# Gate and up weights of two column tiles in one load, and two products side by side

## The chip, the cores and the metric

The kernel runs on one core of one Trainium2 chip. The metric is the device time of one execution in microseconds (us). The engines are called as in the profile: PE multiplies matrices, PEld is its loading of stationary operands, DVE, ACT and POOL work on vectors, SP issues the DMA transfers.

## The reference

One layer of a decoder over 2048 tokens of 1024 numbers: a projection, two groups of attention heads (a softmax group and a stick-breaking group), an output projection, and then a gated feed-forward network. The part that the change touches is that network:

```
f = rmsnorm(h, norm_ffn)
gate = einsum("bsd,df->bsf", f, w_gate)      # 1024 -> 2816
up   = einsum("bsd,df->bsf", f, w_up)        # 1024 -> 2816
h = h + einsum("bsf,fd->bsd", silu(gate) * up, w_down)
return rmsnorm(h, norm_final)
```

All of it is in float32. The kernel reaches that precision by splitting each operand into a high and a low part and adding three products.

## The kernel before, in words

The 2048 tokens are four blocks of 512. Each block passes four stages: P projects it, A is its attention, D its output projection, F its feed-forward network. Blocks 0 and 1 run F one at a time (`ffn`, L974); blocks 2 and 3 share one (`ffn_pair`, L1105), which has loads and products of its own and is not touched.

The code does not issue instructions. It records them as tasks, and `Plan.order` (L295) then writes the order of every engine by playing the tasks through a table of costs: whenever an engine is free, the ready task with the smallest key goes next. The key is a rank and then the place in the recording. Every instruction is issued from one helper, so all rows of the profile have the line L479; they are told apart by the names of their tiles. The order is fixed before the run: an engine whose next instruction must wait does not take the one behind it.

The ranks (L74 to L91) put the feed-forward network of block 0 beside the attention of blocks 2 and 3, at rank 2 like the attention of block 3 but later in the recording: its products (`ps_gu`, `ps_d`) fill the places where no product of the attention (`ps_s`, `pt`, `ot`, `po`) is ready. Block 1 follows, with the output projections of blocks 2 and 3 (`ps_t`, `ps_o`) between its steps; then the pair of blocks 2 and 3 (`ps_m`). What reads a sum out of the matrix engine's memory gets a key smaller by three (`ACC_FIRST`, L88).

The sums stand in eight banks. The attention reserves five of them while it has work (L49 to L51); the tiles of `acc_tile` (L796) share the others. They open in the order of recording, with one liberty: a tile may open ahead of up to ten that were recorded before it, unless one of those or itself is marked as one of a pair (L333 to L334).

`ffn` goes over the 22 column tiles of 128 columns, two at a time. For a tile, `gate_up` (L978) loads 1024 rows by 128 columns of the gate weights (`raw`, three buffers), splits them in two halves into high and low parts (`whi` on ACT, `wlo` on DVE, five buffers each), and adds 24 matmuls into one sum (`ps_gu`): eight row chunks, three products each. Then it does the same with the up weights. From the two sums come the sigmoid (ACT, `sg`), two multiplications (DVE, `sg`), the high part of the result (ACT, `hh`) and the low part (POOL, `hl`). After both tiles `down` (L932) adds, for each of eight output tiles, three matmuls of the first column tile and three of the second (`ps_d`, 48 in all), and DVE adds the sum to the block's accumulator (`acc`).

Of the kernel before, what the change touches and what calls it, by code (L numbers as in the profile page):

```python
# [12 lines left out]
F32 = mybir.dt.float32  # L13
F32R = mybir.dt.float32r
I32 = mybir.dt.int32
AF = mybir.ActivationFunctionType
ALU = mybir.AluOpType
# [4 lines left out]
P = 128  # L22
# [3 lines left out]
KC = D // P  # L26
TB = 512
# [31 lines left out]
SG_BUFS = 4  # L59
# [423 lines left out]
def layer(ctx, tc, x, positions, inv_freq, norm_mix, w_in, q_latent_norm, w_uq,  # L483
# [4 lines left out]
    def f32(ap):  # L488
        return ap.bitcast(F32)
# [23 lines left out]
    plan = Plan()  # L513
# [30 lines left out]
    def split_w(raw, hi, lo):  # L544
        plan.scalar.activation(hi, raw, AF.Copy)
        plan.vector.tensor_tensor(out=lo, in0=raw, in1=f32(hi), op=ALU.subtract)

    def mm3(ps, sh, sl, mh, ml, start, stop):
        plan.tensor.matmul(ps, lhsT=sh, rhs=mh, start=start, stop=False)
        plan.tensor.matmul(ps, lhsT=sh, rhs=ml, start=False, stop=False)  # L550
        plan.tensor.matmul(ps, lhsT=sl, rhs=mh, start=False, stop=stop)


    with ExitStack() as s:

        def planned(name, bufs):
            p = PlanPool(plan, s.enter_context(tc.tile_pool(name=name, bufs=bufs)), bufs)
            p.psum = False
            return p
# [8 lines left out]
        sp, tp, op, accp = [PlanPool(plan, psum, n) for n in (S_B, TP_B, O_B, None)]  # L568
# [227 lines left out]
        def acc_tile(shape, dtype, name, pair=False):  # L796
            tile_ = accp.tile(shape, dtype, tag="acc", name=name)
            tile_.base.pair = pair
            return tile_
# [12 lines left out]
        ew = planned("c_wk", 2)  # L812
# [21 lines left out]
        def weights(src, shape, parts=2):  # L834
            raw = wr.tile(shape, F32, tag="raw", name="raw")
            if isinstance(src, list):
                for i, part in enumerate(src):
                    plan.sync.dma_start(raw[:, i], part)
            else:
                plan.sync.dma_start(raw, src)  # L840
            res = []
            n = shape[1] // parts
            for i in range(parts):
                a = wp.tile([P, n] + shape[2:], F32R, tag="hi", name="whi")
                z = wp.tile([P, n] + shape[2:], F32R, tag="lo", name="wlo")
                split_w(raw[:, i * n:(i + 1) * n], a, z)
                res.append((a, z))
            return res
# [83 lines left out]
        def down(accs, order, hts, dws):  # L932

            for at in order:
                for dh in range(2):
                    ds_ = slice(dh * 512, (dh + 1) * 512)
                    for n in at:
                        ts_ = slice(n % BT * P, (n % BT + 1) * P)
                        ps = acc_tile([P, 512], F32, "ps_d")
                        for i in range(2):  # L940
                            hh, hl = hts[i][n // BT]
                            mm3(ps, hh[:, ts_], hl[:, ts_], dws[i][dh][0], dws[i][dh][1], i == 0, i == 1)
                        plan.vector.tensor_tensor(out=accs[n][:, ds_], in0=accs[n][:, ds_], in1=ps, op=ALU.add)

        def down_weights(c):
            return [weights(w_down[0, i * P:(i + 1) * P, :], [P, D]) for i in (c, c + 1)]

        def load_accs(blocks):
            accs = []
            for n, b in enumerate(blocks):  # L950
                for t in range(BT):
                    pool, tag = (apool, f"acc{t}") if n == 0 else (kv, "kv"[t % 2])
                    a = pool.tile([P, D], F32, tag=tag, name="acc")
                    plan.sync.dma_start(a, d_h[b * TB + t * P:b * TB + (t + 1) * P, :])
                    accs.append(a)
            return accs

        def last_norm(blocks, accs, order):
            pool, tag = (kv, "v") if blocks == [1] else (wr, "raw")
            gfin = pool.tile([P, D], F32, tag=tag, name="gfin")  # L960
            plan.sync.dma_start(gfin, norm_final.unsqueeze(0).broadcast_to([P, D]))
            for n in order:
                a = accs[n]
                so = small.tile([P, 2], F32, tag="so", name="so")
                for g in range(2):
                    squares(a[:, g * 512:(g + 1) * 512], so[:, g:g + 1])
                plan.vector.tensor_tensor(out=so[:, 0:1], in0=so[:, 0:1], in1=so[:, 1:2], op=ALU.add)
                ro = small.tile([P, 1], F32, tag="ro", name="ro")
                rstd_chain(small, so[:, 0:1], 1, D, ro)
                plan.vector.scalar_tensor_tensor(out=a, in0=a, scalar=ro, in1=gfin, op0=ALU.mult, op1=ALU.mult)  # L970
                g = blocks[n // BT] * BT + n % BT
                plan.sync.dma_start(out[0, g * P:(g + 1) * P, :], a)

        def ffn(b, between):  # L974

            fh, fl = sources[b]

            def gate_up(c):  # L978
                pss = []
                for src in (w_gate, w_up):  # L980
                    ws = weights(src[0, :, c * P:(c + 1) * P].rearrange("(c p) n -> p c n", p=P), [P, KC, P])
                    ps = acc_tile([P, TB], F32, "ps_gu")
                    for k in range(KC):
                        a, z = ws[k // 4]
                        mm3(ps, a[:, k % 4, :], z[:, k % 4, :], fh[k], fl[k], k == 0, k == KC - 1)
                    pss.append(ps)
                hh = hp.tile([P, TB], F32R, tag="hh", name="hh")
                hl = hp.tile([P, TB], F32R, tag="hl", name="hl")
                sg = ew.tile([P, TB], F32, tag="sg", name="sg", bufs=SG_BUFS)
                plan.scalar.activation(sg, pss[0], AF.Sigmoid)  # L990
                plan.vector.tensor_tensor(out=sg, in0=pss[0], in1=sg, op=ALU.mult)
                plan.vector.tensor_tensor(out=sg, in0=pss[1], in1=sg, op=ALU.mult)
                plan.scalar.activation(hh, sg, AF.Copy)
                plan.gpsimd.tensor_tensor(out=hl, in0=sg, in1=f32(hh), op=ALU.subtract)
                return [(hh, hl)]

            accs = []
            for c in range(0, NF, 2):
                hts = [gate_up(c), gate_up(c + 1)]
                dws = down_weights(c)  # L1000
                accs = accs or load_accs([b])
                down(accs, [[n] for n in range(BT)], hts, dws)
                for f in between.get(c // 2, ()):
                    f()
            plan.rank += NORM_LATE
            last_norm([b], accs, range(BT))
            plan.rank -= NORM_LATE
# [479 lines left out]
        for what in ORDER:  # L1487
            kind, blocks, between, rank = what[0], what[1], what[2] if len(what) > 2 else {}, RANKS["PADF".index(what[0])]
            rank = what[3] if len(what) > 3 else rank
            plan.rank = rank  # L1490
            steps = {}
            for at, other in between.items():
                todo = out_proj(int(other[1])) if other[0] == "D" else pair_steps
                for i, f in zip(at if isinstance(at, tuple) else (at,) * len(todo), todo):
                    steps.setdefault(i, []).append(f)
            if kind == "P":
                project(blocks, [f for fs in steps.values() for f in fs])
            elif kind == "A":
                plan.dense = False
                attention(blocks)  # L1500
                plan.dense = True
            elif isinstance(blocks, tuple):
                ffn_pair(blocks, ops, rest)
            else:
                sources[blocks], todo = ffn_input(blocks, t_tags)
                for f in todo:
                    f()
                ffn(blocks, steps)
# [26 lines left out]
```

## Time and profile before

| | us |
|---|---|
| median of 3 runs | 2981.82 (2981.56 to 2983.75) |
| the profiled execution | 2980.0 |
| its span | 2978.2 |
| PE busy in the span | 2938.2 (99%) |
| DVE busy | 2313.0 (78%) |
| ACT busy | 1779.5 (60%) |
| POOL busy | 514.4 (17%) |

The span is what the profile covers; the execution's own time is 1.8 us longer. A busy PE is one with a matmul under way, and a matmul is counted longer than the distance to the next one's start, so gaps shorter than that do not show as idle time.

### The profile page before, as it was taken

To read this page: it belongs to the slowest core of one execution; us is meant where nothing else is said; L and a number is where in the kernel's file an instruction comes from. 1 tells how busy PE (TensorE), PEld (TensorE's weight loads), DVE (VectorE), ACT (ScalarE), POOL (GpSimd) and SP (SyncE) were. 2 spreads that over 40 slices of the span, in tenths; PEclk is the share of its full clock that TensorE was granted. 3 is DMA by queue.
4 is the path that set the end of the run, shared out by engine and by line. 5 is a ranking of instruction groups with operands and counts; after the bars stand their busy time and mean duration, and the time that the engine had idled before them with its cause. 6 is when DMAs were issued, how large, how long until landed. Compare 5 with 4: busy or idle time off the path is not lost.

```text
span 2978.2 us, 46737 instructions
## 1 busy us (share of the span) xinstructions
PE 2938.2 (99%) x16308; PEld 2521.4 (85%) x16308; DVE 2313.0 (78%) x4448; ACT 1779.5 (60%) x3834; POOL 514.4 (17%) x487
## 2 busy tenths in 40 slices
PE   8999999999999999999999999999999999999998
PEld 7989889988888888888888888888887888888887
DVE  6668888886889879798979797555758777777777
ACT  6568878775767778777777786444534332233323
POOL 0011222220213213141414131000003101000101
PEclk9999999999999999999999999999999999999999
DMA  7988876669743445334333354546533311111212
GB/s 217 282 269 259 248 228 204 189 195 280 229 122 120 128 128 158 117 121 140 116 114 114 104 168 153 176 141 196 173 95 117 121 57 57 43 57 43 69 45 85
DMA packets 403426, 437.73 MB, mean 147 GB/s; under 512 B 76875, under 2 KB 296054, under 8 KB 403190
## 3 DMA queue, kind: packets, MB, share of 16 engines
q1 hardware_dynamic: 403190, 434.74, 47.8%
q8 instruction: 129, 2.11, 0.3%
q14 instruction: 107, 0.88, 0.1%
HBM read 350.78 MB, written 83.89 MB: 146 GB/s over the span
## 4 chain that ended last, share of the span: by engine, by line
PE 88%; DVE 5%; DMA 3%; ACT 2%; issue 1%; SPq 0%; POOL 0%; POOLq 0%; ACTq 0%; DVEq 0%
PE ps_gu L479 15%; PE ps_d L479 15%; PE ps_m L479 14%; PE ps_s L479 10%; PE ot L479 9%; PE pt L479 7%; PE ps_q L479 5%; PE ps_o L479 4%; PE ps_v L479 3%; PE ps_lat L479 2%; PE ps_t L479 1%; PE po L479 1%; DVE wlo L479 1%; DVE tb L479 1%; DVE acc L479 1%
## 5 line engine op out<-in xcount | busy, mean ns | idle before, releaser
L479 ACT ACTIVATE whi<-raw 128x512 fp32r<-128x512 f32 (+1 forms) x726 | 447.7, 627 | 574.8 <-PE ps_d L479 204.9
L479 DVE TENSOR_TENSOR wlo<-raw,whi 128x512 fp32r<-128x512 f32 (+1 forms) x726 | 515.0, 720 | 229.3 <-ACT whi L479 223.8
L479 POOL TENSOR_TENSOR p<-p,tb 128x512 f32<-128x512 f32 (+3 forms) x320 | 327.0, 1023 | 594.9 <-DVE tb L479 562.5
L479 DVE TENSOR_TENSOR pl<-pt,ph 128x512 fp32r<-128x512 f32 (+1 forms) x576 | 366.9, 651 | 45.7 <-ACT ph L479 42.8
L479 ACT ACTIVATE ph<-pt 128x512 fp32r<-128x512 f32 (+1 forms) x576 | 318.3, 580 | 132.3 <-PE pt L479 117.2
L479 PE MATMUL ps_s<-k,q 128*128 128x512 f32 (+3 forms) x1280 | 379.7, 374 | 3.0 <-DVE tb L479 3.0
L479 PE MATMUL pt<-diagonal,p 128*128 128x128 f32 x2176 | 358.8, 274 | 0.9 <-DVE pl L479 0.9
L479 PE MATMUL ps_m<-fop,whi 128*128 128x512 f32 (+1 forms) x1254 | 357.0, 373 | 0.0
L479 DVE TENSOR_TENSOR acc<-acc,ps_d 128x512 f32<-128x512 f32 x352 | 235.9, 682 | 71.1 <-PE ps_d L479 69.7
L479 PE MATMUL ps_gu<-th,whi 128*128 128x512 f32 x704 | 282.4, 401 | 0.0
L479 PE MATMUL ps_gu<-tl,whi 128*128 128x512 f32 x704 | 281.8, 400 | 0.0
L479 PE MATMUL ps_gu<-th,wlo 128*128 128x512 f32 x704 | 280.9, 399 | 0.0
L479 PE MATMUL ps_d<-whi,hh 128*128 128x512 f32 x704 | 277.5, 394 | 1.4 <-ACT hh L479 1.4
L479 PE MATMUL ps_d<-wlo,hh 128*128 128x512 f32 x704 | 277.2, 394 | 0.0
L479 PE MATMUL ps_d<-whi,hl 128*128 128x512 f32 x704 | 271.1, 393 | 0.0
L479 PEld LDWEIGHTS pt<-diagonal,p 128*128 128x128 f32 x2176 | 255.8, 141 | 14.3 <-issue 1.1
L479 PEld LDWEIGHTS ps_m<-fop,whi 128*128 128x128 f32 x1254 | 226.5, 188 | 44.8
L479 PEld LDWEIGHTS ps_s<-k,q 128*128 128x128 f32 x1280 | 222.8, 189 | 33.9 <-DVE tb L479 5.1
L479 DVE TENSOR_TENSOR_SCAN tb<-ps_s,tb,p 128x512 f32<-128x512 f32 x192 | 244.7, 1277 | 5.2 <-ACT ps_s L479 2.8
L479 PE MATMUL ot<-pl,v 128*128 128x256 f32 (+1 forms) x1152 | 244.5, 292 | 0.3
L479 PE MATMUL ot<-ph,v 128*128 128x256 f32 (+1 forms) x1152 | 233.6, 283 | 3.9 <-ACT ph L479 3.7
L479 DVE TENSOR_REDUCE m<-ps_s 128x1 f32<-128x512 f32 (+2 forms) x320 | 188.6, 605 | 58.4 <-PE ps_s L479 57.6
(215 smaller groups left out, 6062.5 us busy)
## 6 DMA issues: line engine op xcount, KB each, us to landing
raw<-in_w_gate SPq DMA_DIRECT2D x66, 512.0 KB, 4.0
raw<-in_w_up SPq DMA_DIRECT2D x66, 512.0 KB, 3.8
raw<-in_w_down SPq DMA_DIRECT2D x66, 512.0 KB, 4.0
raw<-in_w_o SPq DMA_DIRECT2D x64, 512.0 KB, 4.3
raw<-in_w_in SPq DMA_DIRECT2D x48, 512.0 KB, 5.6
q<-d_mq SPq DMA_DIRECT2D x64, 256.0 KB, 5.2
q<-d_sbq SPq DMA_DIRECT2D x64, 256.0 KB, 4.9
k<-d_mk SPq DMA_DIRECT2D x32, 512.0 KB, 5.3
```

Of the source, the lines that this page charges most:

```text
L479: getattr(getattr(nc, t.engine), t.method)(*args, **kwargs)
```

## The change

For two neighbouring column tiles the gate weights come in two loads of 512 rows by 256 columns instead of two of 1024 rows by 128 columns. Each load is split in two parts of two row chunks. Two sums, marked as a pair, are open at once: for each row chunk three matmuls go into the first and three into the second. Then the same is done for the up weights. So the order of a pair of tiles is gate, gate, up, up, where it was gate, up, gate, up. The number of loads, their bytes, the number of matmuls and of vector instructions stay the same; the loads' contiguous rows in memory are 1024 bytes long where they were 512.

```diff
--- before.py
+++ after.py
@@ -975,28 +975,37 @@
 
             fh, fl = sources[b]
 
-            def gate_up(c):
-                pss = []
-                for src in (w_gate, w_up):
-                    ws = weights(src[0, :, c * P:(c + 1) * P].rearrange("(c p) n -> p c n", p=P), [P, KC, P])
-                    ps = acc_tile([P, TB], F32, "ps_gu")
-                    for k in range(KC):
-                        a, z = ws[k // 4]
-                        mm3(ps, a[:, k % 4, :], z[:, k % 4, :], fh[k], fl[k], k == 0, k == KC - 1)
-                    pss.append(ps)
+            def products(src, c):
+
+                pss = [acc_tile([P, TB], F32, "ps_gu", True) for _ in range(2)]
+                for k2 in range(0, KC, 4):
+                    ws = weights(src[0, k2 * P:(k2 + 4) * P, c * P:(c + 2) * P].rearrange("(c p) n -> p c n", p=P),
+                                 [P, 4, 2 * P])
+                    for k in range(k2, k2 + 4):
+                        a, z = ws[(k - k2) // 2]
+                        for i, ps in enumerate(pss):
+                            ns = slice(i * P, (i + 1) * P)
+                            mm3(ps, a[:, k % 2, ns], z[:, k % 2, ns], fh[k], fl[k], k == 0, k == KC - 1)
+                return pss
+
+            def gated(ps_g, sg):
+                plan.scalar.activation(sg, ps_g, AF.Sigmoid)
+                plan.vector.tensor_tensor(out=sg, in0=ps_g, in1=sg, op=ALU.mult)
+
+            def hidden(ps_u, sg):
                 hh = hp.tile([P, TB], F32R, tag="hh", name="hh")
                 hl = hp.tile([P, TB], F32R, tag="hl", name="hl")
-                sg = ew.tile([P, TB], F32, tag="sg", name="sg", bufs=SG_BUFS)
-                plan.scalar.activation(sg, pss[0], AF.Sigmoid)
-                plan.vector.tensor_tensor(out=sg, in0=pss[0], in1=sg, op=ALU.mult)
-                plan.vector.tensor_tensor(out=sg, in0=pss[1], in1=sg, op=ALU.mult)
+                plan.vector.tensor_tensor(out=sg, in0=ps_u, in1=sg, op=ALU.mult)
                 plan.scalar.activation(hh, sg, AF.Copy)
                 plan.gpsimd.tensor_tensor(out=hl, in0=sg, in1=f32(hh), op=ALU.subtract)
                 return [(hh, hl)]
 
             accs = []
             for c in range(0, NF, 2):
-                hts = [gate_up(c), gate_up(c + 1)]
+                sgs = [ew.tile([P, TB], F32, tag="sg", name="sg", bufs=SG_BUFS) for _ in range(2)]
+                for ps, sg in zip(products(w_gate, c), sgs):
+                    gated(ps, sg)
+                hts = [hidden(ps, sg) for ps, sg in zip(products(w_up, c), sgs)]
                 dws = down_weights(c)
                 accs = accs or load_accs([b])
                 down(accs, [[n] for n in range(BT)], hts, dws)
```

Three places show how the instructions move. The first is PE in block 1 (no attention is left), where the products of column tiles 6 and 7 end and the `ps_d` products begin. In these rows `ps_gu_26237` is the up sum of tile 7 before; `hh_26206` and `hl_26211` are the result of tile 6 and `hh_26285` that of tile 7. Before:

```order
L479 MATMUL ps_gu_26237<-th_24930,wlo_26182 128x512
L479 MATMUL ps_d_26275<-whi_26195,hh_26206 128x512
L479 MATMUL ps_d_26275<-wlo_26203,hh_26206 128x512
L479 MATMUL ps_d_26275<-whi_26195,hl_26211 128x512
L479 MATMUL ps_d_26280<-whi_26217,hh_26206 128x512
L479 MATMUL ps_d_26280<-wlo_26222,hh_26206 128x512
L479 MATMUL ps_d_26280<-whi_26217,hl_26211 128x512
L479 MATMUL ps_d_26288<-whi_26195,hh_26206 128x512
L479 MATMUL ps_d_26288<-wlo_26203,hh_26206 128x512
L479 MATMUL ps_d_26275<-whi_26235,hh_26285 128x512
L479 MATMUL ps_d_26275<-wlo_26243,hh_26285 128x512
```

The change, at the same place; `ps_gu_26196` and `ps_gu_26203` are the up sums of tiles 6 and 7, `hh_26272` and `hl_26278` the result of tile 6, `hh_26276` that of tile 7:

```order
L479 MATMUL ps_gu_26196<-tl_24966,whi_26174 128x512
L479 MATMUL ps_gu_26196<-th_24939,wlo_26179 128x512
L479 MATMUL ps_gu_26203<-th_24939,whi_26174 128x512
L479 MATMUL ps_gu_26203<-tl_24966,whi_26174 128x512
L479 MATMUL ps_gu_26203<-th_24939,wlo_26179 128x512
L479 MATMUL ps_d_26280<-whi_26194,hh_26272 128x512
L479 MATMUL ps_d_26280<-wlo_26205,hh_26272 128x512
L479 MATMUL ps_d_26283<-whi_26216,hh_26272 128x512
L479 MATMUL ps_d_26283<-wlo_26221,hh_26272 128x512
L479 MATMUL ps_d_26286<-whi_26194,hh_26272 128x512
L479 MATMUL ps_d_26286<-wlo_26205,hh_26272 128x512
L479 MATMUL ps_d_26289<-whi_26216,hh_26272 128x512
```

Before, the first `ps_d` products use the result of tile 6, whose sums ended 48 matmuls earlier. Now both up sums end within the last six matmuls, and the first `ps_d` product uses the result of the one that ended three matmuls before the other.

The second is DVE at the same place: the multiplications by which tiles 6 and 7 go from sums to result. Before (tile 7):

```order
L479 TENSOR_TENSOR wlo_26243<-raw_26146,whi_26235 128x512
L479 TENSOR_TENSOR sg_26241<-ps_gu_26197,sg_26241 128x512
L479 TENSOR_TENSOR wlo_26260<-raw_26146,whi_26255 128x512
L479 TENSOR_TENSOR sg_26241<-ps_gu_26237,sg_26241 128x512
L479 TENSOR_TENSOR wlo_26282<-raw_26188,whi_26273 128x512
L479 TENSOR_TENSOR acc_24843<-acc_24843,ps_d_26275 128x512
```

The change:

```order
L479 TENSOR_TENSOR wlo_26239<-raw_26147,whi_26234 128x512
L479 TENSOR_TENSOR wlo_26255<-raw_26147,whi_26250 128x512
L479 TENSOR_TENSOR sg_26190<-ps_gu_26196,sg_26190 128x512
L479 TENSOR_TENSOR sg_26201<-ps_gu_26203,sg_26201 128x512
L479 TENSOR_TENSOR wlo_26274<-raw_26185,whi_26269 128x512
L479 TENSOR_TENSOR acc_24858<-acc_24858,ps_d_26280 128x512
```

Before, the multiplication with the gate sum of tile 7 stood ahead of the last split of the down weights, and one multiplication followed the last `ps_gu`. Now two multiplications with up sums stand one behind the other.

The third is PE in block 0, beside the attention, at the same passage of column tiles 14 and 15. Before (`ps_gu_20385` is the up sum of tile 15, `hh_20188` the result of tile 14; `ot`, `ps_s` and `po` belong to the attention):

```order
L479 MATMUL ps_gu_20385<-th_11374,whi_20037 128x512
L479 MATMUL ps_gu_20385<-tl_11398,whi_20037 128x512
L479 MATMUL ot_20339<-pl_20500,v_20088 128x256
L479 MATMUL ot_20339<-pl_20500,v_20088 128x128
L479 MATMUL ps_gu_20385<-th_11374,wlo_20230 128x512
L479 MATMUL ps_d_20514<-whi_20171,hh_20188 128x512
L479 MATMUL ps_d_20514<-wlo_20237,hh_20188 128x512
L479 MATMUL ps_s_20520<-k_20137,q0_19619 128x512
L479 MATMUL ps_s_20520<-k_20137,q1_19631 128x512
L479 MATMUL ps_s_20520<-kr_691,qr_18636 128x512
```

The change (`ps_gu_21216` and `ps_gu_21248` are the up sums of tiles 14 and 15, `hh_21555` the result of tile 14):

```order
L479 MATMUL ps_gu_21216<-th_11338,wlo_21182 128x512
L479 MATMUL ps_gu_21248<-th_11338,whi_21131 128x512
L479 MATMUL ot_21513<-ph_21539,v_21233 128x256 x2
L479 MATMUL ps_s_21550<-k_21295,q0_20763 128x512
L479 MATMUL ps_s_21550<-k_21295,q1_20780 128x512
L479 MATMUL ps_gu_21248<-tl_11355,whi_21131 128x512
L479 MATMUL ps_gu_21248<-th_11338,wlo_21182 128x512
L479 MATMUL ps_d_21562<-whi_21227,hh_21555 128x512
L479 MATMUL ps_d_21562<-wlo_21340,hh_21555 128x512
L479 MATMUL ps_d_21568<-whi_21324,hh_21555 128x512
L479 MATMUL ps_s_21570<-k_21295,q0_20763 128x512
```

Here too the first `ps_d` product now uses a result of which the sum ended a few rows earlier; two products of the attention on `ot` and two on `ps_s` stand between.

## Rows read from the trace of the kernel before

**Rows 1.** The page's head: busy time, share of the span, instructions.

```profile
span 2978.2 us, 46737 instructions
...
PE 2938.2 (99%) x16308; PEld 2521.4 (85%) x16308; DVE 2313.0 (78%) x4448; ACT 1779.5 (60%) x3834; POOL 514.4 (17%) x487
```

**Rows 2.** The page's chain of work that ended last, by engine.

```profile
PE 88%; DVE 5%; DMA 3%; ACT 2%; issue 1%; SPq 0%; POOL 0%; POOLq 0%; ACTq 0%; DVEq 0%
```

**Rows 3.** Table of stretches: length, PE, PEld, DVE, ACT, POOL busy, PEclk, DMA.

```profile
740.00:820.00 80.00, 77.08 (x518) 67.09 (x518) 67.70 (x153) 61.17 (x144) 16.58 (x18) 0.98 0.72 230
790.00:800.00 10.00, 8.34 (x43) 5.80 (x42) 10.00 (x18) 8.21 (x19) 5.60 (x5) 0.88 0.23 67
820.00:1700.00 880.00, 879.19 (x5383) 767.64 (x5382) 749.64 (x1468) 660.15 (x1419) 226.61 (x214) 1.00 0.41 124
1700.00:1760.00 60.00, 58.69 (x339) 48.77 (x340) 59.71 (x96) 48.98 (x103) 26.46 (x26) 1.00 0.54 163
1760.00:2250.00 490.00, 489.96 (x2346) 407.83 (x2345) 319.66 (x564) 245.59 (x477) 48.59 (x43) 1.00 0.52 157
2250.00:2310.00 60.00, 56.48 (x253) 46.11 (x252) 48.18 (x67) 24.38 (x46) 22.87 (x16) 1.00 0.32 97
2256.00:2260.00 4.00, 2.56 (x12) 1.80 (x11) 4.00 (x6) 0.63 (x1) 2.62 (x2) 1.00 0.79 243
```

**Rows 4.** Timeline in block 1, all engines: start, duration, instruction, [idle before <-releaser].

```profile
2185.67 0.39 PE L479 MATMUL ps_gu<-th,wlo 128*128 128x512 f32 x1
2185.89 0.39 PE L479 MATMUL ps_d<-whi,hh 128*128 128x512 f32 x1
...
2186.09 0.69 DVE L479 TENSOR_TENSOR sg<-ps_gu,sg 128x512 f32<-128x512 f32 x1 [1.53 <-PE ps_gu L479]
2186.12 0.39 PE L479 MATMUL ps_d<-wlo,hh 128*128 128x512 f32 x1
...
2186.88 0.63 ACT L479 ACTIVATE hh<-sg 128x512 fp32r<-128x512 f32 x1 [0.33 <-DVE sg L479]
...
2187.59 1.29 POOL L479 TENSOR_TENSOR hl<-sg,hh 128x512 fp32r<-128x512 f32 x1 [9.59 <-ACT hh L479]
2187.71 0.40 PE L479 MATMUL ps_d<-whi,hh 128*128 128x512 f32 x1
```

**Rows 5.** Timeline in block 1, last but one pair of tiles.

```profile
2254.97 0.39 PE L479 MATMUL ps_gu<-th,wlo 128*128 128x512 f32 x1
...
2257.93 0.63 ACT L479 ACTIVATE hh<-sg 128x512 fp32r<-128x512 f32 x1 [2.12 <-DVE sg L479]
2258.61 0.50 PE L479 MATMUL ps_d<-whi,hh 128*128 128x512 f32 x1 [1.44 <-ACT hh L479]
```

**Rows 6.** Timeline of PE in block 1: transposes, then products.

```profile
2104.90 1.03 PE L479 MATMUL ps_t<-diagonal,od 128*128 128x128 f32 x8
2105.69 0.48 PE L479 MATMUL ps_o<-whi,thl 128*128 128x512 f32 x1
```

**Rows 7.** Timeline in block 0, beside the attention, two passages.

```profile
848.96 0.39 PE L479 MATMUL ps_gu<-th,wlo 128*128 128x512 f32 x1
...
851.89 0.66 ACT L479 ACTIVATE hh<-sg 128x512 fp32r<-128x512 f32 x1
...
1274.44 0.39 PE L479 MATMUL ps_gu<-th,wlo 128*128 128x512 f32 x1
...
1276.05 0.63 ACT L479 ACTIVATE hh<-sg 128x512 fp32r<-128x512 f32 x1
```

**Rows 8.** Instructions on `ps_gu`: count, ns min/median/max, first and last start.

```profile
L479 PE MATMUL ps_gu<-th,whi x704: 387/389/504, 784.5 to 2288.9; 128*128 128x512 f32 x176
...
L479 ACT ACTIVATE sg<-ps_gu x44: 578/594/646, 808.7 to 2284.7; 128x512 f32<-128x512 f32 x44
```

**Rows 9.** Groups of ACT's instructions: busy, mean ns of one, idle before.

```profile
L479 ACT ACT_TABLE_LOAD x60 | 77.0, 1283 | 6.2 <-DVE tb L479 4.5 <-PEq L1524 0.7
```

**Rows 10.** The page's DMA issues: count, KB each, us to landing.

```profile
raw<-in_w_gate SPq DMA_DIRECT2D x66, 512.0 KB, 4.0
```

## The prediction

> **What bounds the kernel now.** I read the head of the page first: PE has a matmul under way for 2938.2 of 2978.2 us [rows 1]. The chain of waits agrees: 88% of the span lies on PE [rows 2]. An average over stages hides where there is room, so the table of stretches comes next [rows 3]. The changed products run from 784.5 to 2288.9 us [rows 8]. In the stretch with the attention beside them, 820 to 1700, PE is idle for 0.81 of 880 us; in block 1, 1760 to 2250, for 0.04 of 490. What is left stands at the edges: 2.92 us at 740 to 820, 1.31 at 1700 to 1760, 3.52 at 2250 to 2310. Together that is 8.6 us.
>
> So there is almost nothing to win on PE's waits, and the question is whether the new order makes PE wait. The timeline of a passage without a wait says how the order before avoided it [rows 4]. The last product of a column tile starts at 2185.67. DVE multiplies at 2186.09 (+0.42), ACT copies to `hh` at 2186.88 (+1.21) for 0.63, and PE uses this result at 2187.71 (+2.04). POOL's `hl` is there at 2188.88 (+3.21). PE fills these 2.04 us with products on the other column tile, whose result had been ready for long; eight of them, one each 0.227 us (2185.89 to 2187.71).
>
> **The change part by part.**
>
> *The matmuls themselves.* 2112 `ps_gu` before and after, the same shapes. In the timeline a product follows the other at the same distance whether it goes to the same sum or to the next one (2185.89, 2186.12) [rows 4]: nothing.
>
> *The loads.* As many, with as many bytes. The old form lands in some 4.0 us after its issue [rows 10], and the one who waits for it is ACT, which is busy for only 245.59 of 490 us in block 1 [rows 3]: I take nothing, in gain or in loss. If that cover were gone, a load that is late by its whole landing time would cost 4.0 us once.
>
> *A: the end of a pair of tiles, without attention beside it.* Twelve such passages stand behind the last product of the attention: the last of block 0 and eleven of block 1. Both up sums now end within six matmuls, and the first `ps_d` product needs the result of the first. From the start of that sum's last product to the first `ps_d` product the order has four matmuls, 4 x 0.227 = 0.91 us. The result takes 2.04 [rows 4]. PE waits 1.13 us, unless the order puts other work between. It does so in seven of the twelve: twelve transposes in two, six transposes in four, two products of the next stage in one. Eight transposes take 0.79 us (2104.90 to 2105.69) [rows 6], so six take 0.59 and leave a wait of 0.54, twelve leave none, and the two products leave 0.68. The sum: 5 x 1.13 + 4 x 0.54 + 0.68 = 8.5 us. Behind the wait seven to eight products use the `hh` of the first tile before its `hl` is needed, 1.6 us or more: with 2.04 that is past 3.21, so there is no second wait.
>
> That is with every result at the fast pace [rows 4]. Between 1790 and 2290 there are 24 copies to `hh`. 17 of them start 1.20 to 1.22 us after their last product, and 7 later, up to +2.96 [rows 5]; these 7 are late by 6.6 us together, 0.28 for each of the 24. Before, the other tile's products hid most of that; the latest was not hidden [rows 5], and PE stood for 1.44 us. Now nothing hides it: between 0 and 12 x 0.28 = 3.3 us more. I take the middle, 1.6. A is 10.1, between 8.5 and 11.8.
>
> *B: the same passage beside the attention.* Ten of these. Of the 20 copies to `hh` there, one in the middle starts 1.61 us after its last product, the latest 2.93 [rows 7], the earliest at the fast pace [rows 4]. With 0.63 for the copy and 0.20 to PE, the result is there after 2.44 us (2.04 to 3.76). The order has, between the last product of the first up sum and the first `ps_d`, work of the attention and products that take, at the distances of the timeline, 5.4, 4.7, 2.4, 2.0, 2.4, 3.3, 4.8, 1.6, 4.8 and 2.4 us. The waits at 2.44 are 0.4 and 0.8, 1.2 in sum; at 2.04 0.4, at 3.76 8.2. I take 1.2, as the row in the middle has it.
>
> *C: banks.* While the attention has work, three banks are left for these sums. Two gate sums hold two of them until sigmoid (0.59) [rows 8] and multiplication (0.69) have read them, some 0.42 + 0.59 + 0.1 + 0.69 + 0.2 = 2.0 us after their last product. The first up sum can take the third bank, the second must wait for the first gate sum, and the order has 2.3 to 4.7 us of PE work up to there: no wait. If the third bank is taken (by an output projection), each up sum waits for one gate sum; against 2.0 us the ten passages then lack 4 to 6 us, and twice that if the sigmoid stands in ACT's queue. Between 0 and 12; I take 2, since mostly a bank should be free.
>
> *D: the start.* Sums in pairs may not open ahead of others. Before, fourteen products of the first gate sum stand between the attention's in 784.5 to 790; now the first one comes after that place, while PE is short of work there (1.66 us idle in 790 to 800, and the clock at 0.88 [rows 3]). Up to 14 x 0.227 = 3.2 us of filling is gone. I take half, 1.6.
>
> *E: what comes back.* The waits of 8.6 us at the edges may shrink: DVE and ACT get more time per product, and ACT's order has 42 table loads for 60, as the sigmoids now come in twos: 18 x 1.283 = 23.1 us of ACT [rows 9]. ACT bounds nothing here (660.15 of 880 us busy) [rows 3], so PE can win at most its own 8.6 us of waits. Between -8.6 and 0; I take -2, as most of these waits are for data, not for ACT.
>
> The sum: 10.1 + 1.2 + 2 + 1.6 - 2 = +12.9 us. On the profiled execution of 2980.0 that is 2992.9; the median of the runs shown is 1.8 above it, so I forecast 2995. The bounds: 8.5 + 0.4 + 0 + 0 - 8.6 = 0.3, and 11.8 + 8.2 + 12 + 3.2 + 0 = 35.2, that is 2982 to 3017.
>
> **The rivals.**
>
> *PE runs dry beside the attention.* By the order 960 `ps_gu` and 307 `ps_o` stand ahead of the attention's last product, where 1053 and 384 stood: 170 matmuls, 170 x 0.227 = 38.6 us of PE work moved behind it. For the rival: DVE is busy for 749.64 of 880 us there [rows 3], and if that sets the attention's pace, the attention ends when it did, and PE has lacked those 38.6 us: 2995 + 38 = 3033. Against it: the attention goes first wherever it is ready, so with less beside it and 18 table loads fewer it should end earlier. It decides by when the last `ot` starts: about 1760 as before, or 1730.
>
> *The waits are hidden after all.* Something that I count as late is not, as products run on [rows 4] at 0.227 us wherever a result is ready: 2982. Against it stands the passage where one late `hh` stopped PE at this very place [rows 5].
>
> *Faster.* ACT's 23.1 us of table loads stand in the attention's chain; without them the 5.0 us of PE's waits in 740 to 1760 [rows 3] go and those of 2250 to 2310 halve, 6.8 in all. It wins only if A stays under that, so if the order's other work covers most of the passages and leaves under 2 us of waits: 2982 - 6.8 + 2 = 2977. Against it: in five of the twelve passages there is no other work.
>
> *The clock.* The granted clock is 0.88 where PE was idle for 1.66 of 10 us: 1.2 us of full speed lost [rows 3]. If each of 12 to 22 new waits did so, 14 to 26 us would come on top: 3009 to 3021. Against it the wait of 1.44 us [rows 5] left the clock at 1.00 (2256 to 2260) [rows 3], and the new ones are shorter and lie further apart.
> The Trainium skill, "TensorE: Matmul & The Clock Gate", section "A second HAM failure mode: psum-queue depth-cycling", tells of a kernel in which PE idled briefly between groups of matmuls so often that its clock swung between its two levels, 1.2 and 2.4 GHz. By that rule this change would pay for the clock at each passage, by the trace it doesn't.
>
> **How the numbers follow.** The forecast with its own range of 2988 to 3017 gets 0.65, the same mechanism with its waits mostly given back (2982 to 2988) 0.05, hidden waits 0.09, PE dry 0.10, faster 0.07, the clock 0.04. A measurement of this kernel can tell about 0.2%, 6 us, from no change. Faster: 0.07. Within 6 us: 0.09 + 0.05 = 0.14. Slower: 0.79. The range of 2980 to 3018 leaves out the dry PE, most of faster, and a part of the clock, some 0.17.
>
> **What would show it.** In the changed kernel's timeline at the twelve passages: an idle time of PE of 0.5 or 1.1 us ahead of the first `ps_d`, released by ACT's `hh`; two `sg` multiplications one behind the other on DVE. PE idle in the stretch of block 1: 8 to 12 us for 0.04. The last `ot` some 30 us earlier. The granted clock at 1.00 throughout block 1. If PE's idle time in block 1 stays under 2 us, A is wrong and with it the forecast; if it is right and the time is 3030, look beside the attention.

## The result and the profile after

The changed kernel takes 3035.9 us (median of 5 runs, 3033.4 to 3037.1) where the kernel before took 2983.8 beside it (5 runs, 2981.6 to 2984.9): ratio 1.0178, 95% interval 1.0165 to 1.0191. I had forecast 2995, and 3018 as the upper end. It is slower, as I had said, but by 52 us and not by 13.

The head of the page after, which answers [rows 1]:

```profile
span 3031.7 us, 46771 instructions
...
PE 2952.3 (97%) x16308; PEld 2529.8 (83%) x16308; DVE 2312.9 (76%) x4448; ACT 1757.1 (58%) x3816; POOL 510.3 (17%) x487
```

PE has the same 16308 instructions. Its idle time is up from 40.0 to 79.4 us, and its busy time by 14.1 us: the same work took longer under way. The stretches of the changed kernel say where, against [rows 3] (length, PE, PEld, DVE, ACT and POOL busy, granted clock, DMA share, GB/s):

```profile
740.00:820.00 80.00, 74.55 (x509) 64.00 (x508) 67.88 (x153) 60.28 (x142) 17.51 (x19) 1.00 0.74 231
820.00:1700.00 880.00, 878.41 (x5406) 766.49 (x5404) 761.74 (x1483) 654.27 (x1433) 238.40 (x225) 1.00 0.40 123
1820.00:2300.00 480.00, 441.31 (x1961) 361.33 (x1960) 271.65 (x467) 198.61 (x380) 43.00 (x38) 0.96 0.47 147
1940.00:1950.00 10.00, 10.00 (x38) 8.12 (x37) 4.30 (x10) 5.42 (x14) 1.01 (x1) 0.79 0.39 121
2100.00:2110.00 10.00, 10.00 (x43) 8.18 (x43) 3.53 (x7) 2.75 (x6) 0.00 (x0) 0.94 0.37 116
2170.00:2180.00 10.00, 9.82 (x37) 7.48 (x37) 8.04 (x17) 6.81 (x12) 0.00 (x0) 0.69 0.64 177
2280.00:2290.00 10.00, 6.68 (x26) 5.56 (x27) 7.88 (x19) 4.45 (x10) 4.52 (x4) 0.66 0.48 137
```

Beside the attention nothing happened: 1.59 us idle of 880, where 0.81 was. In block 1 PE is idle for 38.7 of 480 us, and the mean clock there is 0.96, with four places below 1.00. The last instruction on `po` tells that the attention did end early, at 1784.37 in the changed kernel,

```profile
1784.37 0.60 PE L479 MATMUL po<-diagonal,os 128*128 128x128 f32 x4
```

and at 1821.20 in the kernel before:

```profile
1821.20 0.60 PE L479 MATMUL po<-diagonal,os 128*128 128x128 f32 x4
```

That is 36.8 us earlier, with the 38.6 us of products moved behind it: +1.8 net. So all but some 2 us of the 53.5 between the two spans are lost after the attention. (The prediction has the last `ot` of the kernel before at about 1760; it starts at 1819.8, and at 1783.1 in the changed kernel.) PE's waits in that stretch of the changed kernel, by what ended them (us in total, times, longest):

```profile
PE ps_t L479 <- DVE ht L479: 14.5, 4, 7.4
PE ps_t L479 <- DVE od L479: 14.1, 2, 7.1
PE ps_d L479 <- ACT hh L479: 9.8, 8, 1.4
```

The waits that I forecast are the last row. The two above are 28.6 us that stand nowhere in my sum: transposes for the next blocks, on rows (`od`) of the output projection and on rows (`ht`) of the pair stage's input. The first of them, in a timeline of the changed kernel, all engines:

```profile
1931.14 0.39 PE L479 MATMUL ps_o<-whi,thl 128*128 128x512 f32 x1
1931.48 1.28 DVE L479 TENSOR_TENSOR hx<-hx,ps_o 128x512 f32<-128x512 f32 x2
...
1935.96 0.63 ACT L479 ACTIVATE junk<-od 128x512 bf16<-128x512 f32 x1
...
1936.97 1.01 POOL L479 TENSOR_TENSOR rd<-rc_v,minus_half 128x4 f32<-128x4 f32 x1 [2.12 <-DVE rc_v L479]
...
1938.01 1.68 DVE L479 TENSOR_SCALAR od<-od,rd 128x512 f32<-128x512 f32 x4 [1.12 <-POOL rd L479]
1938.55 1.97 PE L479 MATMUL ps_t<-diagonal,od 128*128 128x128 f32 x8 [7.02 <-DVE od L479]
...
1940.17 0.77 PE L479 MATMUL ps_gu<-th,whi 128*128 128x512 f32 x1
...
1940.74 0.63 PE L479 MATMUL ps_gu<-tl,whi 128*128 128x512 f32 x1
1941.17 0.63 PE L479 MATMUL ps_gu<-th,wlo 128*128 128x512 f32 x1
```

After the output projection the squares of two `hx` and four `od` go through ACT, POOL makes the factor `rd`, DVE scales `od`, and only then PE can transpose. PE stands for 7.02 us with 96 `ps_gu` products behind the transposes in its queue. Afterwards the products follow each other at 0.43 us for the 0.227 of [rows 4]: half speed, the lower of the clock's two levels. The same chain in the kernel before takes as long, and nobody notices it:

```profile
1925.75 0.39 PE L479 MATMUL ps_o<-whi,thl 128*128 128x512 f32 x1
...
1932.30 1.01 POOL L479 TENSOR_TENSOR rd<-rc_v,minus_half 128x4 f32<-128x4 f32 x1 [2.51 <-DVE rc_v L479]
1933.81 1.67 DVE L479 TENSOR_SCALAR od<-od,rd 128x512 f32<-128x512 f32 x4
...
1934.13 0.39 PE L479 MATMUL ps_gu<-th,whi 128*128 128x512 f32 x1
1934.43 1.18 PE L479 MATMUL ps_t<-diagonal,od 128*128 128x128 f32 x8
```

From the last `ps_o` to the transposes it is 8.7 us in the kernel before and 7.4 in the changed one. But before, PE's order had 37 `ps_gu` products in between, 37 x 0.227 = 8.4 us, where the changed order has none. The planner's rule for sums marked as pairs (the test on `pair` in `closed`) keeps a marked sum from opening ahead of any sum that was recorded earlier, and the transposes' sums were. That is theory H (held products) of the experiments. The rivals: that the side by side order itself makes the loss, that the new loads do, or that it lies beside the attention.

### The profile page after: what moved, and what is told of

It reads as the page before. It is cut to its first block, busy times and chain, and to the rows that moved or that the text cites. A ratio compares the mean times of both kernels' runs of the same rounds, so it can differ in the third digit from the quotient of the medians.

```text
span 3031.7 us, 46771 instructions
## 1 busy us (share of the span) xinstructions
PE 2952.3 (97%) x16308; PEld 2529.8 (83%) x16308; DVE 2312.9 (76%) x4448; ACT 1757.1 (58%) x3816; POOL 510.3 (17%) x487
## 4 chain that ended last, share of the span: by engine, by line
PE 87%; DMA 4%; DVE 4%; ACT 3%; issue 1%; SPq 0%; POOL 0%; ACTq 0%; POOLq 0%; DVEq 0%
PE ps_gu L479 16%; PE ps_d L479 15%; PE ps_m L479 14%; PE ps_s L479 10%; PE ot L479 8%; PE pt L479 7%; PE ps_q L479 5%; PE ps_o L479 4%; PE ps_v L479 2%; PE ps_lat L479 2%; PE ps_t L479 1%; PE po L479 1%; DVE wlo L479 1%; ACT whi L479 1%; DMA raw<-in_w_o 1%
## 5 line engine op out<-in xcount | busy, mean ns | idle before, releaser
L479 PE MATMUL ps_d<-whi,hh 128*128 128x512 f32 x704 | 278.9, 396 | 11.8 <-ACT hh L479 11.6
```

The source lines that it names most:

```text
L479: getattr(getattr(nc, t.engine), t.method)(*args, **kwargs)
```

## The experiments

All times are medians of several runs, each set beside runs of the kernel before on the same chip.

**The change in block 1 alone, and in block 0 alone.** `gate_up` of before stays for the other block (here `b == 1`, in the second kernel `b == 0`):

```
+                if b == 1:
...
+                else:
+                    hts = [gate_up(c), gate_up(c + 1)]
```

> The change in block 1 alone, block 0 as before. Theory H (held products): since the changed sums are marked as pairs, none of them may open ahead of an earlier sum; in block 1 the transposes of the next blocks' rows stand between them, their inputs come late, and PE stands for 6 to 7 us at four places. All of that lies in block 1, so 3030 to 3036 us, and the four waits on od and ht are seen again. Rival P (what I priced: the ends of pairs, banks beside the attention, the start): the loss is spread, and block 1 alone gives 11 to 15 us, 2995 to 3000.

> The change in block 0 alone, block 1 as before. Theory H: nothing is held in block 0 for long, as it stands beside the attention; 2982 to 2990 us, and PE's idle time in block 1 is as before. The last attention product starts some 36 us earlier all the same. Rival P, with the banks and the start dearer than I put them: 3000 us or more.

Measured: block 1 alone 3033.5 us (ratio 1.0162, 1.0148 to 1.0176), block 0 alone 2989.0 (1.0016, 1.0007 to 1.0024), against 2984.1. Block 1 carries 49.4 us and block 0 4.9. The spread-out rival is gone. With block 0 alone the last row on `po` starts at 1785.89, 35 us earlier than before, and PE is idle for 2.5 us of 1820 to 2300, where it was 1.5 before: both as theory H has it. PE's waits in 1820 to 2300 with block 1 alone are like those of the changed kernel:

```profile
PE ps_t L479 <- DVE od L479: 15.5, 2, 8.4
PE ps_t L479 <- DVE ht L479: 15.0, 3, 8.7
PE ps_d L479 <- ACT hh L479: 9.8, 8, 1.4
```

**The mark alone.** Old loads, old order of products:

```
-                    ps = acc_tile([P, TB], F32, "ps_gu")
+                    ps = acc_tile([P, TB], F32, "ps_gu", b == 1)
```

> The old loads and the old order of products; only the mark of a pair is set on the gate and up sums of block 1. Theory H: the mark alone makes the four long waits, 28 us, and the clock falls after each, some 10 to 13 us more: 3018 to 3027 us; no waits at the ends of the pairs. Rival S (the side by side order or the new loads make the loss): the mark does nothing, 2982 to 2986 us.

Measured: 3020.7 us (1.0118, 1.0102 to 1.0133), 36.7 more than before. The loads and the recorded order of the products are the old ones; one argument makes 70% of the loss. The waits of PE in 1820 to 2300:

```profile
PE ps_t L479 <- DVE od L479: 14.2, 2, 7.1
PE ps_t L479 <- DVE ht L479: 13.3, 5, 6.2
```

No wait on `hh` is among them. What the change in block 1 costs beyond the mark is 49.4 - 36.7 = 12.7 us.

**The change without the mark in block 1.**

```
-                pss = [acc_tile([P, TB], F32, "ps_gu", True) for _ in range(2)]
+                pss = [acc_tile([P, TB], F32, "ps_gu", b == 0) for _ in range(2)]
```

> The changed kernel with the mark taken off the sums of block 1; loads and side by side order stay. Theory H: the four waits on od and ht go and the clock stays at 1.00; what is left is the waits at the ends of the pairs (11.6 us measured in the changed kernel) and about 2 us before block 1: 2992 to 3000 us. Rival S: 3028 to 3036 us.

Measured: 3000.4 us (1.0050, 1.0037 to 1.0062), just above the upper edge of what H expected. It is 16.3 us over the kernel before beside it, where the changed kernel is 52.1 over: 35.8 less, close to the 36.7 that the mark alone costs. The long waits are gone; what is left in 1820 to 2300 is mostly the ends of the pairs, and the clock is at 1.00:

```profile
PE ps_d L479 <- ACT hh L479: 7.8, 6, 1.4
PE ps_t L479 <- DVE ht L479: 2.6, 4, 1.0
PE ps_gu L479 <- ACT whi L479: 1.5, 3, 0.5
PE ps_t L479 <- DVE od L479: 0.5, 1, 0.5
...
1820.00:2300.00 480.00, 467.62 (x2119) 382.40 (x2119) 293.71 (x494) 206.70 (x395) 50.34 (x42) 1.00 0.49 155
```

**The mark kept, the transposes later.** If held products are harmless once the transposes' inputs are ready, moving the transposes must help as much as taking the mark off:

```
-D2_AT = (0, 0, 1, 1, 1, 1, 1, 2, 2, 3)
-D3_AT = (1, 2, 3, 3, 4, 4, 4, 5, 5, 5)
-H_AT = (5, 5, 8, 8)
+D2_AT = (0, 0, 1, 1, 1, 1, 2, 2, 2, 3)
+D3_AT = (1, 2, 3, 3, 4, 4, 5, 5, 5, 5)
+H_AT = (6, 6, 9, 9)
```

> The changed kernel, marks and all, with the transposes of the second halves and of the four chunks put one pair of column tiles later in the program (three tables of places). Theory H: their inputs are then ready when PE comes to them, so the four waits of 6 to 7 us go although the sums may still not overtake: 2992 to 3001 us, as without the mark. Rival: the transposes wait for their inputs wherever they stand (their rows are loaded only once buffers come free), and the waits stay: 3020 to 3036 us.

Measured: 3004.4 us (1.0064, 1.0052 to 1.0077), between the two, and nearer to H. Three of the four long waits are gone. One stayed as it was, and for it the rival was right: the eight loads of that group's `ht` are issued only at 2279.37, when PE is already at the last transposes of the group before (2279.41). That a buffer held them back is not shown.

```profile
2286.06 0.69 PE L479 MATMUL ps_t<-diagonal,ht 128*128 128x128 f32 x2 [6.05 <-DVE ht L479]
```

**Useless products in the waits.** To tell idle time from the clock, 28 products into a sum that nobody reads were put ahead of each of the four groups of transposes (the calls are left out):

```
+        def filler(n):
+            ps = acc_tile([P, TB], F32, "ps_x")
+            fh = sources[1][0]
+            for i in range(n):
+                plan.tensor.matmul(ps, lhsT=fh[i % KC][:, :P], rhs=fh[i % KC], start=i == 0, stop=i == n - 1)
```

> The changed kernel with 28 useless products (6.4 us at 0.227 us each) ahead of each of the four groups of transposes that wait 6 to 7 us; they go to a sum that nobody reads. If the fall of the granted clock after the waits is a cost of its own, 112 products more make the kernel faster: the products take the place of the waits, and the clock stays at 1.00; 3022 to 3030 us. Rival: the slow stretch after the waits has another cause (the late inputs themselves), or the products come on top: 3036 to 3062 us.

Measured: 3031.6 us (1.0152, 1.0138 to 1.0166), between the two ranges expected. It is 46.0 us over the kernel before beside it, where the changed kernel is 52.1 over (1.0165 to 1.0191). The two intervals just touch, so the gain of 6 us is likely and not certain. The profiles, one of each kernel, are clearer. The stage begins and ends here:

```profile
1790.31 0.49 PE L481 MATMUL po<-diagonal,os 128*128 128x128 f32 x3
...
2343.96 0.50 PE L481 MATMUL ps_m<-fop,whi 128*128 128x512 f32 x1 [0.54 <-ACT whi L481]
```

From the attention's last instruction to the pair stage's first it takes 553.7 us, against 559.9 in the changed kernel (1784.37 to 2344.28): 6.3 less, with 112 x 0.227 = 25.4 us of products more. The waits of over 0.4 us on `od` and `ht` sum to 4.4 us here and to 28.4 there, which is 24.0 less. So 25.4 - 24.0 + 6.3 = 7.7 us came back because products ran faster. The stretches after the waits:

```profile
1940.00:1950.00 10.00, 8.39 (x42) 6.77 (x41) 4.19 (x12) 7.18 (x20) 1.71 (x2) 1.00 0.55 193
2100.00:2110.00 10.00, 9.24 (x46) 7.47 (x45) 4.90 (x11) 3.03 (x8) 1.01 (x1) 1.00 0.52 162
2170.00:2180.00 10.00, 9.67 (x37) 6.93 (x38) 8.07 (x19) 6.08 (x11) 0.00 (x0) 0.66 0.69 197
```

Two of them stay at 1.00 where they had 0.79 and 0.94; the fourth place, not shown, stays at 1.00 too. The third still falls to 0.66. There twelve transposes run behind the products, and the next twelve wait 2.07 us and take 3.17 for 1.48:

```profile
2166.57 1.48 PE L481 MATMUL ps_t<-diagonal,ht 128*128 128x128 f32 x12
...
2170.12 3.17 PE L481 MATMUL ps_t<-diagonal,ht 128*128 128x128 f32 x12 [2.07 <-DVE ht L481]
```

The rows at the lower clock say the same. In the changed kernel, PE's work behind the four waits begins at 0.50:

```profile
1938.55:1944.12 5.57, 5.57 (x17) 4.73 (x18) 2.80 (x7) 2.90 (x8) 0.00 (x0) 0.50 0.58 191
2097.91:2101.14 3.23, 3.23 (x12) 2.94 (x13) 2.49 (x7) 1.57 (x4) 0.00 (x0) 0.50 0.77 219
2167.47:2176.23 8.76, 8.43 (x24) 5.53 (x25) 7.03 (x16) 4.92 (x8) 0.00 (x0) 0.50 0.69 199
2283.32:2288.87 5.55, 5.55 (x21) 4.64 (x22) 3.91 (x9) 2.02 (x4) 3.39 (x3) 0.50 0.26 91
```

That is 22.8 us of work at the lower level, where it takes about twice as long (0.43 us for 0.227): by estimate 11 us are lost. In the filled kernel 6.6 us of work are left at 0.50, all at the third place, which loses 3. The difference, 8 us, is what came back. So the clock is a cost of its own, some 11 us in the changed kernel.

**The new loads, one sum after the other.** The 24 products of a tile's sum all come before the next tile's, unmarked:

```
+                wss = [weights(src[0, k2 * P:(k2 + 4) * P, c * P:(c + 2) * P].rearrange("(c p) n -> p c n", p=P),
+                               [P, 4, 2 * P]) for k2 in range(0, KC, 4)]
+                for i, ps in enumerate(pss):
+                    ns = slice(i * P, (i + 1) * P)
+                    for k in range(KC):
+                        a, z = wss[k // 4][k % 4 // 2]
+                        mm3(ps, a[:, k % 2, ns], z[:, k % 2, ns], fh[k], fl[k], k == 0, k == KC - 1)
```

> The new loads (512 rows for two column tiles), but the four sums of a pair one after the other (gate, gate, up, up) and unmarked. Theory: the loads cost nothing, and with the first tile's up sum done 5.4 us ahead of the second's no hh is late: 2978 to 2987 us. Rival L (the loads cost something, in landing time or in buffers held longer): 2992 us or more.

Measured: 2983.0 us, ratio 0.9995 (0.9986 to 1.0004): no change. Within that interval the loads cost nothing and bring nothing, although the page counts 358369 DMA packets for 403426.

**Gate products ahead of the down products.** Side by side, unmarked in block 1:

```
...
+                sgs = sgs or gates(c)
                 hts = [hidden(ps, sg) for ps, sg in zip(products(w_up, c), sgs)]
+                sgs = gates(c + 2) if b == 1 and c + 2 < NF else []
                 dws = down_weights(c)
```

> Side by side, unmarked in block 1, and there the gate products of the next pair are recorded ahead of this pair's down products. If the waits on hh at the ends of the pairs are what is left without the mark, they are hidden behind 10.9 us of products: 9 to 10 us under the kernel without the mark, 2988 to 2993 us. Rival: something else in the side by side order is left (the weights' splits, banks): 2997 to 3003 us.

Measured: 2985.9 us (0.9998, 0.9990 to 1.0007), 0.3 over the kernel before beside it, where the kernel without this step is 16.3 over: 16 less, and I expected 9 to 10. Of the waits on `hh` in 1820 to 2300, 7.8 us without it, 0.9 is left. The longest waits now are:

```profile
PE ps_d L479 <- DVE wlo L479: 1.8, 1, 1.8
PE ps_t L479 <- DVE od L479: 1.2, 1, 1.2
PE ps_d L479 <- ACT hh L479: 0.9, 1, 0.9
```

All listed waits in that stretch fell from 12.4 to 5.0 us, which is 7.4 of the 16; where the rest came from is not resolved.

**Block 0.** Two kernels ask where its 4.9 us come from: the mark off in both blocks, and block 0 as before with block 1 as in the last experiment.

```
-                pss = [acc_tile([P, TB], F32, "ps_gu", True) for _ in range(2)]
+                pss = [acc_tile([P, TB], F32, "ps_gu") for _ in range(2)]
```

> The changed kernel with the mark taken off in both blocks, side by side order kept. The changed block 0 alone cost 4.9 us. If that is the mark (the first products held at the start, sums held beside the attention), this kernel is 3 to 5 us under the one unmarked in block 1 alone: 2995 to 2998 us. Rival (two up sums that wait for banks beside the attention, or the end of the pairs there): no difference, 2999 to 3003 us.

> Block 0 as before; block 1 side by side, unmarked, with the next pair's gate products ahead of this pair's down products. A candidate for the best version: if the 4.9 us of block 0 go as they came, 2985.9 - 4.9 = 2981 us, 2977 to 2985; a gain over the kernel before would have to come from its waits on PE in block 1, 3.5 us at most. Rival: block 1's new form still costs 3 us or more, and the kernel is at 2986 to 2990.

Measured: 2992.8 us (1.0032, 1.0020 to 1.0044) without any mark, 8.5 over the kernel before beside it, where the kernel with the mark in block 0 is 16.3 over. That is 7.8 less, more than the 3 to 5 that I expected and more than the whole 4.9 of block 0; the two intervals overlap a little, so part of it is noise. PE is busy for 114.56 of 120 us in 700 to 820, where the changed kernel has 112.37:

```profile
700.00:820.00 120.00, 114.56 (x719) 98.45 (x718) 93.00 (x208) 82.43 (x194) 16.47 (x18) 1.00 0.79 247
```

This speaks for the mark at the start rather than for banks. The mark is also what moved most of the 170 products behind the attention: without it the last row on `po` starts at 1813.05, and 34 products are moved.

Block 0 as before with the new block 1 takes 2984.0 us (1.0000, 0.9991 to 1.0008), in the range that I expected. But the 4.9 us of block 0 did not come back visibly: with the changed block 0 the ratio was 0.9998 already. The intervals are too wide to tell 2 or 3 us. No version beats the kernel before, and there is little to win in block 1: in the kernel before PE is idle for 1.5 us of 1820 to 2300.

## Why the prediction was wrong

The step that failed is D, "Sums in pairs may not open ahead of others". I had the rule and priced it at one place, the start of block 0, with 1.6 us. It holds wherever a marked sum stands behind another sum, and in block 1 the transposes of the output projections and of the pair stage's input stand between the products. In A I counted such transposes at six ends of pairs as filling that is ready when PE comes to it, and there they were. For the other groups I did not ask whether their inputs are ready; the four long waits stand at nothing in the sum. The trace of before had the answer, the chain from `ps_o` to `od` of 8 us shown above; PE never waits for it there, so its waits do not lead to it. The mark alone costs 36.7 us in block 1: 26 us in four long waits, and the rest by estimate the clock behind them. At the start itself, the trace of before has twelve products of the first gate sum in 784.5 to 790, not the fourteen of D.

A, the ends of the pairs: the mechanism was right; that the size fits is in part luck. I forecast 10.1 us. The page after has 11.6 on `hh`, in ten waits, and 12.7 us is what block 1 costs beyond the mark:

```profile
L479 PE MATMUL ps_d<-whi,hh 128*128 128x512 f32 x704 | 278.9, 396 | 11.8 <-ACT hh L479 11.6
```

The places are the forecast ones: five of 1.01 us where I had 1.13, one of 0.74 where I had 0.68, none behind twelve transposes. The four with six transposes have 1.44 or 1.45, where I had 0.54. A timeline of one:

```profile
1860.28 1.38 DVE L479 TENSOR_TENSOR sg<-ps_gu,sg 128x512 f32<-128x512 f32 x2 [0.91 <-PE ps_gu L479]
...
1860.77 0.82 PE L479 MATMUL ps_t<-diagonal,od 128*128 128x128 f32 x6
1861.27 1.19 ACT L479 ACTIVATE thl<-ps_t,gains 128x256 fp32r<-128x256 f32 x3
...
1862.34 1.16 ACT L479 ACTIVATE hh<-sg 128x512 fp32r<-128x512 f32 x2
1863.03 0.50 PE L479 MATMUL ps_d<-whi,hh 128*128 128x512 f32 x1 [1.45 <-ACT hh L479]
```

The transposes fill PE, but their three copies stand ahead of `hh` on ACT for 1.19 us, which is more than the 0.82 that they filled. That is 3.6 us more at the four places than I took. The 1.6 us that I had added for late results do not show, and the five others are 0.6 us shorter; so the sum came out near. The two `sg` multiplications in a row are as forecast.

B, C, D and one end of a pair make block 0: 4.9 us measured, 4.8 for B, C and D in the sum. That they were split rightly isn't shown, and the interval for block 0 is 2 to 7 us, so the match may be luck; the kernel without marks suggests that D is the largest and more than the 1.6 I took.

E, what comes back: I took 2. The waits of 1.44 and 2.08 us of the kernel before, 3.5 together, are gone as such. ACT has 42 table loads for 60, but so has the kernel at ratio 0.9998: no run shows a gain from them.

The clock: I gave it a chance because of many waits of about 1 us. Those did nothing: cut into stretches of 10 us, block 1 has a clock under 1.00 only at the long waits and right behind them. The long waits brought it, which I had not seen. The Trainium skill, "TensorE: Matmul & The Clock Gate", says in the section "HAM oscillation — how this bites in real kernels" that PE which stands long enough for its inputs starts the next work at the lower clock. This trace agrees: 0.79, 0.94, 0.69 and 0.66 in stretches where PE works behind waits of 6.0 to 7.4 us, 1.00 after 1.45. The section that I cited, on brief and frequent idling, did not bear on this kernel.

"PE runs dry beside the attention" was rejected rightly: the attention's end moved by 36.8 us. Of what would show it, the clock "at 1.00 throughout block 1" and "8 to 12 us" idle there were wrong (0.96, and 38.7), and the waits on `hh` right.

The account: 36.7 (the mark in block 1), 12.7 (the rest of block 1, a difference of two runs) and 4.9 (block 0) are 54.3, against 52.1 measured for the whole. Within the 36.7, the four long waits are 26.1. Behind them the kernel with the mark alone has 22.3 us of PE's work at a granted clock of 0.50, of which half, by estimate 11 us, is lost: together 37.

## What to carry to other kernels

A flag that decides what may overtake is priced at every place where something stands ahead of the flagged work, not only where the change seems to aim: list those places in the new order, and for each ask when its inputs come, from the chain in the old trace, even where no wait shows. Work that fills one engine's wait isn't free if its results then queue ahead of the awaited one on another engine. And after a long wait, count the slow restart too.

## What the runs showed of the hardware

More work made the stage shorter: with 112 useless products in the waits it took 6.3 us less (one profile of each). After a wait of about 7 us, 512-column products ran at 0.43 us apart for 0.227, and 8 transposes took 1.97 us for 1.03 ([rows 6]). Waits of 1.0 to 1.45 us between dense products left the granted clock at 1.00, nine times in one stage. But in the filled kernel a wait of 2.07 us between two groups of twelve transposes was followed by 6.6 us of work at 0.50.
